# Ranks in the delta stage, fetches at the ends of the down projection's chains, and work moved to GpSimd and ScalarE in a hybrid decoder layer

## The chip, the cores and the metric

The kernel runs on 1 core of one Trainium2 chip. The metric is the device time of one execution, in microseconds (us). Engines are named as in the profile: PE is TensorE's matmul side and PEld its weight loads, DVE is VectorE, ACT ScalarE, POOL GpSimd, SP the engine that issues most DMAs. Each engine works through its instructions in one fixed order; an instruction whose operands aren't ready holds up what is behind it on its engine.

## The reference

One layer of a hybrid decoder over 1024 prompt rows and 8 sample rows, D_MODEL 1024, D_FF 2816, all in f32:

```python
h = _rmsnorm(x, norm1_w) * (1 + sc1) + sh1
qkv, gdn_gate, beta_raw, a_raw, sq, sk, sv, ga, gb = _split_in(h @ w_in)
# delta rule, 8 heads of 128, chunks of 64: t_inv = inverse of (I + M) per chunk,
# then a scan over chunks with the state S:
v_new = u_n - w_n @ S
o = qd_n @ S + a_n @ v_new
S = S * last_n + kd_n.T @ v_new
y_a = _gdn_out(o_a, gdn_gate, gdn_onorm_w) @ w_gdn_out
y_b = o_b @ w_swa_out                      # o_b: sliding-window attention
x = x + gt1 * ((sigmoid(ga) * y_a + sigmoid(gb) * y_b) @ w_o)
h2 = _rmsnorm(x, norm2_w) * (1 + sc2) + sh2
gc = _causal_dwconv(h2 @ w_ffn_gate, ffn_conv_w) + ffn_conv_b
x = x + gt2 * ((silu(gc) * (h2 @ w_ffn_up)) @ w_ffn_down)
```

A final RMSNorm follows, and the new states are outputs too.

## The kernel before

Every f32 matmul is made of three: each operand is split into a high part (a rounded copy, made on ACT, L127) and a low part (the rest, made on DVE, L128), and `mm3` issues high by high, low by high and high by low (L178, L179, L180). So each weight that is fetched passes ACT and DVE before PE can use it. Rows stand in three parts of 384, 384 and 264 (`PARTS`) or in quarters of 256 and 260, features in the 128 partitions.

The stages follow one another: modulation and first norm to about 45 us; attention to 430; the delta stage to 1150; the branches (the products with w_swa_out and w_gdn_out, and the sample rows' delta step) to 1330; the output pass (w_o), woven with the second norm and the FFN's operands, to 1445; gate and up to about 1885; down to 2090; the tail with the final norm.

**Order.** The program is written as generators, and `weave` (L1248) gives each one a start and a step: before each piece is written out the priority is set to the stream's start, plus its step for every piece so far. A scheduler then fixes the order on each engine: of what it takes to be ready, the instruction of the lowest priority number goes first. `weave` also says where the next weave begins (`end`).

**Delta stage.** For each head h, `run` (L1924) weaves the inverse (`unit_inverse`, L980), the scan over the chunks (`delta_scan`, L916), the preparation of the next head, and work that only fills: `head_projections` (L797) makes the gate of head h (three tiles) and q, k, v of head h+2 (nine tiles) in two PSUM banks, and `pieces` (L805) draws from one generator that makes first the branch gates (`gates`, L1271; tiles of 24 matmuls in one PSUM bank, taken out on ACT at L1284, written to the DRAM buffers sgb and sga) and then the part of w_swa_out's product that is ready early (`early_out`, L1294). The inverse of a head ends in a chain: L1046 on PE, copies L1048 on ACT, L1051 on PE, L1053 and L1055 on ACT, L1057 on DVE, L1060 on PE, L1061 on ACT, L1064 on PE, L1065 on ACT. A step of the scan is L937 (PE), L938 (DVE), L940 (PE), L942 (ACT), L944 (PE), L953 (DVE), with the outputs at L947 and L948. `early_out` fetches the attention's output (ob) part 2 for itself, and part 0 (`obX`) for the branches; both fetches are split piece by piece on ACT (b1h) and on DVE.

**Branches** (`branches`, L1318). Tiles rotate through five PSUM banks by `next_mm` (`self.turn`). A tile of w_gdn_out's product is multiplied by its gate rows (L1331) and added (L1332); the gate rows are fetched by `gate_part` (L1374) from sga, for the last products into two buffers `sgx`. DVE also makes the sample rows' state updates there (L1207, eight in a row).

**Output pass and second norm.** The loads of w_o (L1431) stand on SP behind those of `gate_part`. `second_norm` (L1462) takes a root on POOL (L123), makes a diagonal on DVE (L1488) and spreads it with PE (L1489). `ffn_states` (L1538) transposes the stored FFN rows (L188). `pair_weights` (L1560) fetches 2 x 2 blocks of an FFN weight and forms the seven operands of Strassen's scheme; its sums (L1572) run on POOL, except for the first blocks of gate and up, on DVE.

**Gate and up** (`ffn_gate_up`, L1636). `conv` (L1657) makes the causal convolution of a gate tile: one multiply with a bias (L1662), then DVE steps (L1664) and the activation.

**Down** (`ffn_down`, L1709). Seven Strassen products of eleven steps each are run in the chains (5, 3), (4, 7), (1), (2) and (6). Within a chain the products go on in the same eight PSUM banks, and `take` (L1763) copies the sums out after each product (L1766, on ACT). `fetch` brings a step's operands 13 steps ahead: DMAs, for most products a sum on POOL (L1737), then the split on ACT and DVE.

## Time and profile before

| | |
|---|---|
| time, median of 3 runs | 2136.81 us (2132.54 to 2142.25) |
| the profiled execution's own time | 2136.28 us |
| its span | 2134.5 us |
| mean granted PE clock | 0.979 |
| PE, DVE, ACT, POOL busy | 96%, 65%, 40%, 25% of the span |
| DMA | 274.95 MB, mean 129 GB/s |

A row of the timeline has the start (us), the duration (us), the engine and line, operation, output and inputs, shape and count; behind it in brackets stand the engine's idle time before that row and what released it. A row of the waits has the total us, the number of times and the longest. Busy time of PE includes the time in which pipelined matmuls overlap, so it says where PE stood still, not how well it was used.

### The profile page before, as it was taken

To read this page: it belongs to the slowest core of one execution; us is meant where nothing else is said; L and a number is where in the kernel's file an instruction comes from. 1 tells how busy PE (TensorE), PEld (TensorE's weight loads), DVE (VectorE), ACT (ScalarE), POOL (GpSimd) and SP (SyncE) were. 2 spreads that over 40 slices of the span, in tenths; PEclk is the share of its full clock that TensorE was granted. 3 is DMA by queue.
4 is the path that set the end of the run, shared out by engine and by line. 5 is a ranking of instruction groups with operands and counts; after the bars stand their busy time and mean duration, and the time that the engine had idled before them with its cause. 6 is when DMAs were issued, how large, how long until landed. Compare 5 with 4: busy or idle time off the path is not lost. (4 is left out here: it accounts for less than half of the span.)

```text
span 2134.5 us, 41210 instructions
## 1 busy us (share of the span) xinstructions
PE 2046.5 (96%) x16245; PEld 1935.3 (91%) x16245; DVE 1393.5 (65%) x2781; ACT 854.7 (40%) x2125; POOL 534.6 (25%) x592
## 2 busy tenths in 40 slices
PE   7999999999899999999989989998999999999898
PEld 4985888899899999999879989898999999999898
DVE  4756667465655736557445575479888788678866
ACT  3655445434244233443343222344343343343443
POOL 1000000020221211212110220003546546545531
PEclk8999999999999999999989999999999999999999
DMA  7256442141332322313166663622333333388972
GB/s 272 86 133 204 141 161 90 49 135 48 76 85 58 83 58 54 89 52 76 48 183 211 213 224 100 182 61 71 109 95 95 110 95 95 120 285 276 317 228 85
DMA packets 301821, 274.95 MB, mean 129 GB/s; under 512 B 59666, under 2 KB 248303, under 8 KB 301612
## 3 DMA queue, kind: packets, MB, share of 16 engines
q1 hardware_dynamic: 296140, 252.49, 38.6%
q0 software_dynamic: 5200, 19.32, 2.6%
q8 instruction: 127, 2.08, 0.4%
q14 instruction: 66, 0.54, 0.1%
q10 hardware_dynamic: 288, 0.52, 0.1%
HBM read 212.54 MB, written 62.12 MB: 129 GB/s over the span
## 5 line engine op out<-in xcount | busy, mean ns | idle before, releaser
L178 PE MATMUL mm<-b1h,wh 128*128 128x384 f32 (+1 forms) x1520 | 499.0, 329 | 5.9 <-ACT gt L1284 4.1
L180 PE MATMUL mm<-b1h,wl 128*128 128x384 f32 (+1 forms) x1520 | 491.4, 325 | 2.1 <-DVE wl L128 2.1
L179 PE MATMUL mm<-b1l,wh 128*128 128x384 f32 (+1 forms) x1520 | 490.8, 323 | 0.0
L178 PEld LDWEIGHTS mm<-b1h,wh 128*128 128x128 f32 x1520 | 287.8, 190 | 15.7 <-ACT gt L1284 6.2
L180 PEld LDWEIGHTS mm<-b1h,wl 128*128 128x128 f32 x1520 | 287.3, 189 | 7.9 <-issue 4.3
L179 PEld LDWEIGHTS mm<-b1l,wh 128*128 128x128 f32 x1520 | 288.0, 189 | 3.8 <-issue 3.5
L127 ACT ACTIVATE wh<-raw 128x1024 fp32r<-128x1024 f32 x83 | 87.0, 1048 | 135.7 <-PE mm L179 75.9
L128 DVE TENSOR_TENSOR wl<-raw,wh 128x1024 fp32r<-128x1024 f32 x82 | 100.8, 1229 | 48.8 <-ACT wh L127 47.9
L179 PE MATMUL mm<-pk,w 128*128 128x260 f32 (+1 forms) x440 | 124.3, 283 | 1.1 <-DVE pk L128 1.1
L178 PE MATMUL mm<-pk,w 128*128 128x260 f32 (+1 forms) x440 | 124.3, 283 | 0.0
L180 PE MATMUL mm<-pk,w 128*128 128x260 f32 (+1 forms) x440 | 124.2, 282 | 0.0
L128 DVE TENSOR_TENSOR w<-ws,w 128x512 fp32r<-128x512 f32 x88 | 74.1, 843 | 37.4 <-ACT w L127 37.4
L1609 ACT COPY bml<-mm 128x256 f32<-128x256 f32 (+1 forms) x132 | 49.2, 374 | 108.5 <-PE mm L180 101.8
L178 PE MATMUL mm<-bmh,w 128*128 128x260 f32 (+1 forms) x320 | 90.4, 283 | 0.9 <-DVE fa L1686 0.9
L180 PE MATMUL mm<-bmh,w 128*128 128x260 f32 (+1 forms) x320 | 90.3, 282 | 0.0
L180 PE MATMUL mm<-b2h,wl 128*128 128x384 f32 (+1 forms) x256 | 83.4, 329 | 4.5 <-DVE wl L128 4.5
L178 PE MATMUL mm<-b2h,wh 128*128 128x384 f32 (+1 forms) x256 | 83.8, 329 | 2.4 <-DVE t L1327 2.4
L179 PE MATMUL mm<-b2l,wh 128*128 128x384 f32 (+1 forms) x256 | 83.9, 328 | 0.4 <-DVE b2l L128 0.4
L179 PEld LDWEIGHTS mm<-pk,w 128*128 128x128 f32 x440 | 82.8, 188 | 1.3 <-DVE pk L128 1.3
L178 PEld LDWEIGHTS mm<-pk,w 128*128 128x128 f32 x440 | 82.8, 188 | 0.3 <-ACT bml L1609 0.2
L180 PEld LDWEIGHTS mm<-pk,w 128*128 128x128 f32 x440 | 83.0, 189 | 0.0
L127 ACT ACTIVATE w<-ws 128x512 fp32r<-128x512 f32 x88 | 55.4, 632 | 49.9 <-PE wv L180 45.0
(648 smaller groups left out, 5984.1 us busy)
## 6 DMA issues: line engine op xcount, KB each, us to landing
raw<-in_w_in_dram SPq DMA_DIRECT2D x60, 512.0 KB
ws<-in_w_ffn_down_dram SPq DMA_DIRECT2D x55, 256.0 KB
raw<-xd SPq DMA_DIRECT2D x47, 258.0 KB
raw<-in_w_ffn_down_dram SPq DMA_DIRECT2D x47, 256.0 KB
raw<-in_w_ffn_gate_dram SPq DMA_DIRECT2D x22, 512.0 KB
raw<-in_w_ffn_up_dram SPq DMA_DIRECT2D x22, 512.0 KB
qst<-in_w_mod_dram SPq DMA_DIRECT2D x16, 512.0 KB
raw<-in_w_mod_dram SPq DMA_DIRECT2D x16, 512.0 KB
```

What stands on the lines that cost most here:

```text
L127: self.nc.scalar.activation(hi, x, AF.Copy)
L128: (eng or self.nc.vector).tensor_tensor(lo, x, hi.bitcast(F32), op=ALU.subtract)
L178: mm(ps, whi, xhi, start=first, stop=False, **kw)
L179: mm(ps, whi, xlo, start=False, stop=False, **kw)
L180: self.last_mm = mm(ps, wlo, xhi, start=False, stop=last, **kw).ins
L1609: self.last_copy = nc.scalar.copy(r[p, i], x[p])
```

## The change

It has nine edits. (1) `weave` counts only streams of step 1 for `end`. (2) In the delta stage the streams of `head_projections`, and for head 6 that of the last gates, start at 100000 instead of 500 or 600, behind the 10000 of the pieces. (3) `early_out` loads ob part 0 at its fourth round instead of ahead of the first. (4) `gate_part` issues the `sgx` loads from POOL's queue. (5) The convolution's first step is an ACT activation. (6) In `ffn_down` fetches don't run in the last two steps of a chain's last product, and the splits of fetches from the 13th on are ordered behind the last copy. (7) `ffn_states` starts at 460 instead of 300. (8) The sums of the first gate block run on POOL. (9) `branches` begins with the first bank of the rotation. Line numbers after the change are one higher from L1303 on, and two or more from L1738 on.

```diff
         for gen, start, step in streams:
             at = tc.cur_priority = p + start
             for _ in gen:
-                if start < 10000:
+                if step == 1:
                     end = max(end, tc.cur_priority)
                 at += step
                 tc.cur_priority = max(at, tc.cur_priority) if step == 1 else at
-            if start < 10000:
+            if step == 1:
                 end = max(end, tc.cur_priority)
         tc.cur_priority = end
 
...
         self.S0, states = [], [self.flat_room(self.b1, "b1", x, 1) for x in "hl"]
         X = {2: self.load_part(self.b1, self.ob, 2, "b1")}
         w = load(0)
-        self.obX = {0: self.load_part(self.b1, self.ob, 0, "b1")}
         for j in range(8):
             s = self.t(self.gt[0], [P, 384], self.gt[1])[:, :n]
             nc.sync.dma_start(s, self.sgb[j][:, lo:lo + n])
...
                 nc.vector.tensor_tensor(s, ps, s, op=ALU.mult)
                 nc.sync.dma_start(self.ubd[j], s)
 
+            if j == 3:
+                self.obX = {0: self.load_part(self.b1, self.ob, 0, "b1")}
             now, w = w, load(j + 1) if j < 7 else None
             if j < 6:
                 self.load_state(j, states[j // 3])
...
 
     def gate_part(self, pool, src, t):
         s = (self.t(pool, [P, 384], "gt") if pool is self.gt[0] else self.t(pool, [P, 384], "sgx", bufs=2))[:, :PARTS[t][1]]
-        self.nc.sync.dma_start(s, src)
+        (self.nc.sync if pool is self.gt[0] else self.nc.gpsimd).dma_start(s, src)
         return s
 
 
...
             e = min(c + n, NP)
             zi, ai = z[i], a[i]
             col = lambda j: fcw[:, j, f + i:f + i + 1]
-            nc.vector.tensor_scalar(ai[:, c:e], zi[:, 2 + c:2 + e], col(2), col(3), op0=ALU.mult, op1=ALU.add)
+            nc.scalar.activation(ai[:, c:e], zi[:, 2 + c:2 + e], AF.Identity, scale=col(2), bias=col(3))
             for j in (0, 1):
                 nc.vector.scalar_tensor_tensor(ai[:, c:e], zi[:, j + c:j + e], col(j), ai[:, c:e],
                                                op0=ALU.mult, op1=ALU.add)
...
                 1: ((0, 0, 1), (1, 1, 1)), 2: ((0, 1, 1), (1, 1, -1)), 6: ((1, 1, 1),)}
         steps = [(i, g) for c in chains for i in c for g in range(G)]
         ready, waiting = {}, ([], [])
+        self.took = None
         less = []
 
         def fetch(s):
...
             room = self.room(tags[s % len(tags)], [P, KC * QW])
             hi, lo = room[:, :n + 512], room[:, n + 512:2 * (n + 512)]
             with ExitStack() as after:
-                if 5 <= s < len(tags):
-                    for ins in (self.last_up, self.last_copy):
-                        after.enter_context(self.tc.issue_after(ins.ins))
+                for ins in (self.last_up, self.last_copy) if 5 <= s < len(tags) else (self.took,) if s >= len(tags) and self.took else ():
+                    after.enter_context(self.tc.issue_after(ins.ins))
                 self.split(hi, lo, raw)
             ready[s] = hi, lo
             if s == 5:
...
         def take(ps, i, p, j):
             self.turn = (self.turn + 1) % KC
             r = self.copies[:, self.turn, :256 + 4 * p]
-            nc.scalar.copy(r, ps)
+            self.took = nc.scalar.copy(r, ps)
             for k, h in enumerate(home[i]):
                 waiting[k].append((r, p, j, *h))
 
         banks = [(self.pmm, "mm", 2), (psum, "wv", 2), (psum, "wy", 2)] * 2 + [(self.pmf, "mm", 1), (psum, "nr", 1)]
         order = [(p, j) for j in range(4) for p in range(2)]
         s = done = 0
+
+        def fetch_to(n):
+            nonlocal done
+            while done < min(n, len(steps)):
+                fetch(done)
+                done += 1
+
         for c in chains[:-1]:
             ps = {(p, j): self.t(pl, [P, 512], tag, bufs=k)[:, :256 + 4 * p] for (p, j), (pl, tag, k) in zip(order, banks)}
             for i in c:
                 for g in range(G):
-                    while done < min(s + len(tags), len(steps)):
-                        fetch(done)
-                        done += 1
+                    if i != c[-1] or g < G - 2:
+                        fetch_to(s + len(tags))
                     for p, j in order:
                         step(s, ps[p, j], p, j, g == 0 and i == c[0], g == G - 1, {"skip_group_check": True} if i != c[0] else {})
                         if g == G - 1:
...
                     s += 1
         for x in waiting[0] + waiting[1]:
             add(*x)
-        while done < len(steps):
-            fetch(done)
-            done += 1
+        fetch_to(len(steps))
         self.ffn_rows(pool, psum)
         tail = self.norm_rows(pool, psum, [2 * P, 3 * P])
         chunks = [[0], [P], [], [], [4 * P, 5 * P], [6 * P, 7 * P, NP], [], []]
...
                     self.squares, self.X, self.wo = {}, {}, []
                     norm = lambda q: self.second_norm(xr, psum, q)
                     self.weave((chain(*(self.output_pass(xr, q) for q in range(4))), 0, 1),
-                               (self.ffn_states(xr, psum), 300, 30),
+                               (self.ffn_states(xr, psum), 460, 30),
                                (chain(norm(0), self.operands(xr, 0, 0)), 250, 10),
                                (chain(norm(1), self.operands(xr, 0, 1)), 490, 20),
                                (chain(norm(2), self.operands(xr, 1, 0)), 730, 120))
                 with S() as left:
                     pool = self.pool("pf", 1, ctx=left)
-                    w = self.pair_weights(pool, self.I["w_ffn_gate"][0], 0, nc.vector)
+                    w = self.pair_weights(pool, self.I["w_ffn_gate"][0], 0)
                     last, ops = norm(3), self.operands(xr, 1, 1)
                     self.weave((chain(islice(last, 3), islice(ops, 1), last, ops), -100, 1))
                     right.close()
...
                     streams = [(self.unit_inverse(pool, psum, h, prep[0]), 0, 1),
                                (self.delta_scan(pool, psum, h, prep), 100, 1)]
                     if h + 2 < H:
-                        streams[1:1] = [(chain(self.pieces(2), self.head_projections(pa, pool, h)), 500, 100)]
+                        streams[1:1] = [(chain(self.pieces(2), self.head_projections(pa, pool, h)), 100000, 100)]
                         streams.append((self.pieces(3), 10000, 100))
                     else:
                         if h + 2 == H:
-                            streams[1:1] = [(chain(self.pieces(3), *(self.delta_gate(pa, pool, i) for i in (h, h + 1))), 500, 1)]
-                        streams.append((self.head_projections(pa, pool, h), 600, 100))
+                            streams[1:1] = [(chain(self.pieces(3), *(self.delta_gate(pa, pool, i) for i in (h, h + 1))), 100000, 100)]
+                        streams.append((self.head_projections(pa, pool, h), 100000, 100))
                     if h + 1 < H:
                         streams.append((self.delta_prepare(pool, psum, h + 1), 250, 1))
                     self.weave(*streams)
...
             pool2, pool = self.pool("p6b", 1, ctx=c), self.pool("p6", 1, ctx=c)
 
             self.psm, more = self.pool("qs", 2, PSUM, ctx=c), self.pool("qb", 2, PSUM, ctx=c)
-            mm, self.mm = self.mm, [self.pmm, self.pmm, self.pmf, more, more]
+            mm, self.mm, self.turn = self.mm, [self.pmm, self.pmm, self.pmf, more, more], -1
             self.branches(pool, pool2)
             self.mm = mm
         cg.close()
```

The change moves instructions on every engine. Three places show how. Each piece is unbroken; the numbers in the names only tell tiles apart.

**PE, the last head's inverse.** tp, T, MR, UZ and W are the inverse's tiles (names 12xxx, L1046 to L1064), rc and vn the scan's, mm_12339 a tile of `early_out`. Before:

```order
L1046 MATMUL tp_12088<-MR_12010,U_1902_11947 32x32 x16
L178 MATMUL mm_12339<-b1h_1987_12296,wh_12312 128x264
L179 MATMUL mm_12339<-b1l_1988_12297,wh_12312 128x264
L180 MATMUL mm_12339<-b1h_1987_12296,wl_12313 128x264
L1051 MATMUL tp_12090<-T_12005,tmp_12089 32x32 x16
L1060 MATMUL tp_12130<-MR_12010,UZ_11948 64x64 x8
L1064 MATMUL tp_12140<-W_4463,UZ_11948 64x64 x8
L940 MATMUL rc_12153<-vn_11914,W_4463 128x128
L178 MATMUL mm_12339<-b1h_1987_12296,wh_12312 128x264
```

After, from the same L1046 on (mm_11700 and mm_11735 are gate tiles, rc_11516 to o_11463 belong to the scan of head 6):

```order
L1046 MATMUL tp_12088<-MR_12010,U_1902_11947 32x32 x16
L940 MATMUL rc_11516<-y_11512,W_4463 128x128
L178 MATMUL mm_11700<-b1h_14_152,wh_11638 128x264
L179 MATMUL mm_11700<-b1l_15_153,wh_11638 128x264
L180 MATMUL mm_11700<-b1h_14_152,wl_11639 128x264
L178 MATMUL mm_11700<-b1h_14_152,wh_11638 128x264
L179 MATMUL mm_11700<-b1l_15_153,wh_11638 128x264
L180 MATMUL mm_11700<-b1h_14_152,wl_11639 128x264
L1051 MATMUL tp_12090<-T_12005,tmp_12089 32x32 x15
L944 MATMUL rc_11520<-s_11518,kd_10802 128x128
L948 MATMUL o_11463<-s_11518,A_10854 128x128
L1051 MATMUL tp_12090<-T_12005,tmp_12089 32x32
```

and at L1060:

```order
L179 MATMUL mm_11735<-b1l_15_153,wh_11731 128x264
L180 MATMUL mm_11735<-b1h_14_152,wl_11732 128x264
L178 MATMUL mm_11735<-b1h_14_152,wh_11731 128x264
L179 MATMUL mm_11735<-b1l_15_153,wh_11731 128x264
L1060 MATMUL tp_12130<-MR_12010,UZ_11948 64x64 x8
L180 MATMUL mm_11735<-b1h_14_152,wl_11732 128x264
L178 MATMUL mm_11735<-b1h_14_152,wh_11731 128x264
L179 MATMUL mm_11735<-b1l_15_153,wh_11731 128x264
```

Before, three matmuls of another stream stand between L1046 and L940; now gate tiles and the last step of head 6's scan stand between its steps.

**ACT, the same place.** b1h are the splits of ob (b1h_1987 part 2, b1h_1992 part 0 before, b1h_2008 part 0 after), gt the gate tiles' way out. Before:

```order
L127 ACTIVATE b1h_1987_12296<-b1l_1988_12297 128x528 x2
L127 ACTIVATE b1h_1992_12316<-b1l_1993_12317 128x768
L127 ACTIVATE wh_12406<-raw_12404 128x1024
L1284 ACTIVATE gt_11818<-mm_11793 128x384
L127 ACTIVATE b1h_1992_12316<-b1l_1993_12317 128x768
L1048 COPY tmp_12089<-tp_12088 32x256 x2
L127 ACTIVATE b1h_1992_12316<-b1l_1993_12317 128x768 x2
L1053 COPY w_1927_12125<-tp_12090 32x256
L1055 COPY W_4463<-tp_12090 32x8x32 x2
L1061 COPY UZ_11948<-tp_12130 64x512
L1065 COPY W_4463<-tp_12140 64x8x64
L942 ACTIVATE s_12155<-rc_12153,c_1887_11877 128x128
```

After:

```order
L1061 COPY UZ_11948<-tp_12130 64x512
L1284 ACTIVATE gt_11760<-mm_11735 128x264
L127 ACTIVATE b1h_1987_12296<-b1l_1988_12297 128x528 x3
L1065 COPY W_4463<-tp_12140 64x8x64
L127 ACTIVATE b1h_1987_12296<-b1l_1988_12297 128x528
L1284 ACTIVATE gt_11789<-mm_11764 128x384
L127 ACTIVATE b1h_2008_12426<-b1l_2009_12427 128x768 x2
L942 ACTIVATE s_12155<-rc_12153,c_1887_11877 128x128
L127 ACTIVATE wh_12392<-raw_12390 128x1024
L1284 ACTIVATE gt_11818<-mm_11793 128x384
L127 ACTIVATE b1h_2008_12426<-b1l_2009_12427 128x768 x2
L942 ACTIVATE s_12168<-rc_12166,c_1887_11877 128x128
```

The copies of the inverse (L1048 stands 10 rows above this piece) are now ahead of the splits of part 0, and these stand ahead of the first two L942 of the last scan.

**SP and POOL, the end of the branches.** On SP before:

```order
L1543 DMA out_dram<-in_state_ffn_conv_dram 8x2816
L1376 DMA sgx_14157<-sga_3915 128x384
L1376 DMA sgx_14190<-sga_3915 128x384
L1376 DMA sgx_14223<-sga_3915 128x264
L1376 DMA sgx_14256<-sga_3915 128x264
L1431 DMA raw_14296<-in_w_o_dram 128x8x128
L1431 DMA raw_14334<-in_w_o_dram 128x8x128
L1431 DMA raw_14370<-in_w_o_dram 128x8x128
```

On SP after:

```order
L1544 DMA out_dram<-in_state_ffn_conv_dram 8x2816
L1432 DMA raw_14296<-in_w_o_dram 128x8x128
L1432 DMA raw_14334<-in_w_o_dram 128x8x128
L1432 DMA raw_14370<-in_w_o_dram 128x8x128
L1415 DMA x_2197_14293<-xT_949 128x256 x6
```

and on POOL after, with the first sums of the FFN's gate weight and the second norm's root (rs):

```order
L1377 DMA sgx_14157<-sga_3915 128x384
L1377 DMA sgx_14190<-sga_3915 128x384
L1377 DMA sgx_14223<-sga_3915 128x264
L1377 DMA sgx_14256<-sga_3915 128x264
L1573 TENSOR_TENSOR ws_15483<-raw_15473,raw_15475 128x512
L1573 TENSOR_TENSOR ws_15485<-ws_15483,raw_15473 128x512
L1573 TENSOR_TENSOR ws_15493<-raw_15473 128x512
L123 TENSOR_TENSOR rs_15356<-rs_15356,mhalf 128x2
```

The loads of w_o no longer have the four gate loads ahead of them, and three weight sums stand ahead of the root on POOL, where before only the root stood.

## The prediction

> **What bounds the kernel now.** I read the page's busy lines first, then busy time in stretches of 50 us, then PE's waits, then the timeline around each place where PE stands idle.
>
> ```profile
> span 2134.5 us, 41210 instructions
> PE 2046.5 (96%) x16245; PEld 1935.3 (91%) x16245; DVE 1393.5 (65%) x2781; ACT 854.7 (40%) x2125; POOL 534.6 (25%) x592
> PE   7999999999899999999989989998999999999898
> ```
>
> PE is busy 96% of the span, so no other engine's total matters. The change removes no matmul and adds none, so all it can win or lose lies in the 2134.5 - 2046.5 = 88 us in which PE is idle, and in slow matmuls behind idle time. About 15 of the 88 us stand in the first slice, ahead of everything that is edited. The rest is spread over places of 0.4 to 5 us. The question of each edit is therefore which of those places it closes, and which it opens.
>
> In the next view a row is a stretch: its length, busy us (instructions) of PE, PEld, DVE, ACT, POOL, then the granted PE clock, the DMA share and GB/s.
>
> ```profile
> 550.00:600.00 50.00, 45.97 (x482) 42.82 (x481) 22.80 (x60) 18.38 (x54) 10.07 (x15) 1.00 0.27 78
> 1100.00:1150.00 50.00, 41.01 (x364) 39.19 (x363) 24.57 (x43) 20.33 (x45) 3.84 (x5) 0.86 0.74 217
> 1450.00:1500.00 50.00, 43.86 (x352) 42.36 (x352) 47.57 (x67) 22.62 (x44) 24.88 (x23) 1.00 0.25 78
> 1700.00:1750.00 50.00, 50.00 (x422) 50.00 (x421) 38.09 (x67) 19.69 (x40) 28.27 (x28) 1.00 0.35 109
> ```
>
> Head 0 of the delta stage loses 4.0 us in its 50, the end of the delta stage 9.0, the start of the FFN 6.1 with DVE at 47.57 of 50. In the middle of the FFN PE never stops.
>
> **The delta stage: the ranks (A and B).** The longest idle time there stands in the last head's inverse, a chain PE, ACT, PE, DVE, PE, ACT, PE, ACT, PE:
>
> ```profile
> 1108.00 1.45 PE L1051 MATMUL tp<-T,tmp 32*32 32x32 f32 x32 [4.15 <-ACT tmp L1048]
> 1112.19 1.94 PE L1060 MATMUL tp<-MR,UZ 64*64 64x64 f32 x16 [2.75 <-DVE MR L1057]
> 1114.80 1.96 PE L1064 MATMUL tp<-W,UZ 64*64 64x64 f32 x16 [0.67 <-ACT UZ L1061]
> 1117.43 0.80 PE L940 MATMUL rc<-vn,W 128*128 128x128 f32 x2 [0.67 <-ACT W L1065]
> ```
>
> That is 4.15 + 2.75 + 0.67 + 0.67 = 8.2 us. By the order of the instructions nothing but three matmuls stands between these steps before, because the last gate tiles were all used up ahead of them; after, dozens of gate matmuls stand between L1046 and L1064. ACT explains the 4.15:
>
> ```profile
> 1104.66 0.84 ACT L127 ACTIVATE b1h<-b1l 128x768 fp32r<-128x768 f32 x1 [2.70 <-DMA b1l<-ob]
> 1107.58 0.75 ACT L1048 COPY tmp<-tp 32x256 f32<-32x256 f32 x2
> 1109.75 0.84 ACT L127 ACTIVATE b1h<-b1l 128x768 fp32r<-128x768 f32 x1 [0.47 <-DMA b1l<-ob]
> ```
>
> The copies of L1048 stood behind splits of the attention's output that waited for their DMA. After the change these splits (the later load of ob part 0) stand behind L1065, but ahead of the first two L942 of the last scan. So the 8.2 us go, and the 2.70 + 0.47 = 3.2 us of waiting for the DMA turn up in the scan, at most. I charge them in full; if the load lands later still, I allow 7.
>
> The idle time has a tail. The same 264-wide matmul takes 0.42 us right behind it and 0.28 us three us later, and the granted clock of this stretch is 0.86, against 1.00 in its neighbours:
>
> ```profile
> 1118.24 0.42 PE L179 MATMUL mm<-b1l,wh 128*128 128x264 f32 x1
> 1120.68 0.28 PE L178 MATMUL mm<-b1h,wh 128*128 128x264 f32 x1
> ```
>
> If the slow clock is half the full one, 0.86 means (1 - 0.86) x 50 / 0.5 = 14 us of it. Of these, 8.2 us were idle; PE lost half of the other 5.8, that is 2.9 us. The Trainium skill ("TensorE: Matmul & The Clock Gate", Part 1) says that the array falls to half its clock after an idle window of about 3.4 us and needs about as long a busy one to come back. This trace agrees in kind behind 4.15 us, though a shorter gap (2.75 us at 1230.23, below) is also followed by a matmul of 0.69 us, where the same shape takes 0.41 and 0.44 in the two rows under it. By the page's figures one slow window of 3.4 us would cost 1.7 us and the sum would be 1.2 us smaller; I keep the 2.9 of the row.
>
> **B: -8.2 - 2.9 + 3.2 = -7.9 us** (from -11.1 to -4).
>
> **A** is heads 0 to 6. Here PE waits mostly for a gate tile's way out of the one PSUM bank that the fillers share:
>
> ```profile
> PE mm L178 <- ACT gt L1284: 4.1, 7, 1.3
> ```
>
> Seven waits, 4.1 us in total, the longest 1.3. They arise where one gate tile follows another with little between. Counted in the order of the instructions, 16 of 39 tiles stand so before and 9 after, because at head 0 projections now alternate with gate tiles. With one wait for a weight's low half,
>
> ```profile
> 546.58 0.45 PE L180 MATMUL mm<-b1h,wl 128*128 128x384 f32 x1 [1.40 <-DVE wl L128]
> ```
>
> 5.5 us are to be had; by the count, 7/16 of them go. **A: -2 us** (from -5 to +6, if the bunched projections wait in their two banks instead).
>
> **Branches (C).** A reset rotation of the five banks and the moved operands:
>
> ```profile
> 1230.23 0.69 PE L180 MATMUL mm<-b2h,wl 128*128 128x384 f32 x1 [2.75 <-DVE wl L128]
> 1237.97 0.41 PE L178 MATMUL mm<-b2h,wh 128*128 128x384 f32 x1 [2.35 <-DVE t L1327]
> 1261.40 0.44 PE L180 MATMUL mm<-b2h,wl 128*128 128x384 f32 x1 [1.74 <-DVE wl L128]
> ```
>
> The first is the same in both orders: the weight's low half stands behind eight state updates on DVE. At the second a tile of 24 matmuls of another part now stands ahead of the one that waits for its bank, so the 2.35 goes. At the third the low half moved ahead on DVE, but other updates still precede it, so I take half. **C: -2.35 - 0.9 = -3.2 us** (from -6 to +2).
>
> **Gate rows through GpSimd, FFN states later (D).**
>
> ```profile
> 1311.00 12.80 SPq L1376 DMA_DIRECT2D sgx<-sga  x4
> 1323.85 2.08 SPq L1431 DMA_DIRECT2D raw<-in_w_o_dram  x3
> 1330.12 0.39 PE L1422 MATMUL mm<-bmh,w 128*128 128x256 f32 x1 [2.06 <-ACT w L127]
> 1342.80 0.39 PE L180 MATMUL mm<-bmh,pk 128*128 128x256 f32 x1 [0.75 <-DVE pk L128]
> 1349.38 0.39 PE L180 MATMUL mm<-bmh,pk 128*128 128x256 f32 x1 [0.64 <-DVE pk L128]
> 1353.58 0.52 PE L188 MATMUL wv<-ident,raw 88*128 88x88 f32 x4 [0.78 <-DMA raw<-in_state_ffn_conv_dram]
> ```
>
> SP sits 12.80 us in four gate loads whose two buffers come free tile by tile, and the first three loads of w_o are queued behind. On POOL the same loads block nothing, since it does nothing at all in this stretch:
>
> ```profile
> 1300.00:1350.00 50.00, 46.55 (x335) 45.92 (x334) 26.79 (x53) 14.99 (x32) 0.00 (x0) 1.00 0.56 158
> ```
>
>  The w_o loads then wait only for their own buffers, some 13 us earlier, and the next ones find the DMA rings emptier. The state's transposes are ranked later, behind more of the output pass. **D: -2.06 - 0.75 - 0.64 - 0.78 = -4.2 us** (from -5 to 0: if POOL brings a gate row late, the tile's bank stays taken, at most the 2.35 us of the bank that DVE kept at 1237.97, and the state's 0.78 stays).
>
> **Weight sums on GpSimd (E).**
>
> ```profile
> 1364.26 0.69 DVE L1572 TENSOR_TENSOR ws<-raw,raw 128x512 f32<-128x512 f32 x1 [6.80 <-DMA raw<-in_w_ffn_gate_dram]
> 1366.89 0.72 POOL L123 TENSOR_TENSOR rs<-rs,mhalf 128x2 f32<-128x2 f32 x1 [105.45 <-issue]
> 1368.12 0.70 PE L1489 MATMUL nr<-dg,ones 128*128 128x256 f32 x2 [2.77 <-DVE dg L1488]
> L1572 POOL TENSOR_TENSOR ws<-raw,raw x20: 1280/1346/1713, 1465.6 to 1843.0; 128x512 f32<-128x512 f32 x20
> ```
>
> DVE stood 6.80 us in front of a sum whose weight was on its way, and the second norm behind it. Now POOL stands there, three sums ahead of the root L123 that the norm needs. The load is queued on SP behind the same stores, which follow PE, so it lands at the same place in the program: the root comes 3 x 1.35 = 4.0 us after the landing, against 1366.89 - 1364.26 = 2.6 us before. PE has 14 more matmuls ahead of L1489 in the new order, 14 x 0.12 = 1.7 us at the 50 us per 422 matmuls of the row 1700. The stall stays at about 2.5 us. **E: 0** (from -2.8 to +3).
>
> **FFN gate and up (F).** The first step of the convolution goes from DVE to ACT.
>
> ```profile
> 1484.67 0.38 PE L178 MATMUL wv<-bml,w 128*128 128x256 f32 x1 [1.60 <-DVE bml L1684]
> 1491.61 0.39 PE L178 MATMUL mm<-bmh,w 128*128 128x260 f32 x1 [0.72 <-DVE fa L1686]
> 1494.93 0.39 PE L178 MATMUL wv<-pk,w 128*128 128x260 f32 x1 [1.38 <-DVE bml L1684]
> L1662 DVE TENSOR_SCALAR fa<-fz,fcw 128x512 f32<-128x512 f32 x4 | 2.1, 537 | 0.0
> L127 ACT ACTIVATE w<-ws 128x512 fp32r<-128x512 f32 x88 | 55.4, 632 | 49.9 <-PE wv L180 45.0
> ```
>
> In the first stretch DVE is nearly full and 1.60 + 0.72 + 1.38 = 3.7 us of PE's idle time end with it. Four steps of 0.54 us leave DVE there, 2.1 us, so I let 2.0 of the 3.7 go. Over the stage 44 x 0.54 = 24 us leave DVE and, at the 632 ns of an activation of this size, 28 us come to ACT. PE covers both: from 1500 on it is full while ACT has 30 us free in 50 (the row 1700). Were that cover gone, a step of 0.63 against 0.54 would lengthen each of 44 chains by 0.1 us, 4 us. **F: -2.0 us** (from -3.7 to +4).
>
> **The down projection (G).**
>
> ```profile
> 1985.46 1.06 ACT L127 ACTIVATE bmh<-bmh 128x1028 fp32r<-128x1028 f32 x1 [2.42 <-POOL bmh L1737]
> 1986.84 0.58 PE L178 MATMUL mm<-pk 128*128 128x256 f32 x1 [4.98 <-ACT bml L1766]
> 2021.60 0.39 PE L178 MATMUL mm<-bml 128*128 128x256 f32 x1 [1.28 <-ACT bml L1766]
> ```
>
> The copies out of PSUM stand behind splits that wait for their fetch. But the 4.98 us fall at the end of product 4, the first of the chain (4, 7), and the edit holds fetches back only in the last product of a chain; before the copies of product 4 the same two splits stand in both orders. At the end of product 7 one split still stands among the copies, now one copy earlier. The names say that the stall at a chain's end goes; the order says that it doesn't. **G: 0** (from -9, the 6.3 shown and a slow tail like B's 2.9, to +5, one more such stall).
>
> **The sum.** -2 - 7.9 - 3.2 - 4.2 + 0 - 2.0 + 0 = -19.3 us. The profiled execution took 2136.28 us (1.8 of it outside the span), 0.5 below the median of 2136.81, so I forecast **2117 us**.
>
> **The rivals.**
>
> - *The down stalls go as well* (chance 0.10). For it: the splits wait for POOL, so a fetch that comes 2.42 us earlier frees the copies. Against it: the order above. 2117 - 9 = 2108.
> - *The stalls move on* (0.18). Engines work in order; what is no longer late lets the next thing be late. The last scan waits 7 us for ob part 0 (B: -4.1), A and C give 0, E costs 3, F gives 0, D half of its 4.2. That is -3.2: 2133. For it: the splits that set L1048 free now stand ahead of L942 on the same ACT; against it: PE has filler in the new order at each place.
> - *Slower: projections ranked last* (0.07). A head makes three gate and nine projection tiles, so 72 over six heads. If they bunch at a head's end behind all other work, each turn waits for a bank as gate tiles do now, 4.1/7 = 0.59 us: 72 x 0.59 = 42, less the 17.3 of the other terms: 2161. From 0.24 us a turn the gain is gone, from 0.39 it is slower by over 0.5%. For it: the rank stands behind even the fillers; against it: two banks instead of one, and orders that hardly differ from head 1 to 5.
> - *The change doesn't do what it says* is counted in G, at nothing.
>
> **How the numbers follow.** The forecast has 0.65, with a range of its own from 2105 to 2130. About 0.5% (10.7 us) is what a measurement of this kernel can tell from no change: faster is below 2126, slower above 2147. Of the 0.65 I put 0.57 below 2126, with the 0.10 of the down stalls and 0.03 of the stalls that move on: 0.70. Slower is 0.07, the rest, 0.23, is the same. For 8 in 10 I leave out the slower rival and the ends of the others: 2103 to 2137.
>
> **What the profile after would show.** B right: no gap over 1 us at L1051 and L1060 of the last head and a granted clock near 1.00 there; wrong: a gap at L940 or L944 ended by ACT s L942. A: the waits for gt fall from seven to about four; wrong: waits of projections for z or th. C: no 2.35 in front of a part's first matmul. D: the w_o loads on SP stand some 13 us ahead of their first use, no gap at L1423. E: the gap of 2 to 3 us at the second norm stays, now ended by POOL. F: DVE under 47 of 50 between 1450 and 1500 in the program's place. G: one stall of about 5 us still in front of product 7. What would make all of it wrong: PE idle above 88 us in total.

## The result and the profile after

The changed kernel takes 2119.37 us (median of 6 runs, 2113.12 to 2124.07) against 2134.27 us of the kernel before beside it (6 runs): a ratio of 0.9922, 95% interval 0.9898 to 0.9946. A second comparison on another chip gave 2118.41 against 2137.03 us, a ratio of 0.9909 (0.9893 to 0.9925). The forecast was 2117 us, or 0.991. The medians differ by 14.9 and by 18.6 us; the two profiled executions, of which all that follows is read, by 2134.5 - 2115.2 = 19.3 us of span. So the size of the gain is known to some 4 us.

The page of the changed kernel:

```profile
span 2115.2 us, 41270 instructions
PE 2041.3 (97%) x16245; PEld 1929.9 (91%) x16245; DVE 1358.7 (64%) x2733; ACT 883.5 (42%) x2169; POOL 535.6 (25%) x602
```

PE's idle time falls from 88.0 to 2115.2 - 2041.3 = 73.9 us, 14.1 less. Its busy time falls by 5.2 us although the matmuls are the same; I take this for time at the slow clock, as the mean granted clock rose from 0.979 to 0.984. Together they make the 19.3 us of the span.

Three of the stretches that the prediction shows, and one in the down projection (us, then busy us of PE, PEld, DVE, ACT, POOL, granted clock, DMA share, GB/s):

```profile
550.00:600.00 50.00, 48.14 (x490) 46.12 (x489) 29.98 (x66) 17.07 (x41) 11.30 (x16) 1.00 0.31 81
1100.00:1150.00 50.00, 45.51 (x343) 43.41 (x340) 27.23 (x49) 19.72 (x42) 7.45 (x10) 1.00 0.90 259
1450.00:1500.00 50.00, 49.27 (x412) 49.06 (x411) 44.87 (x66) 23.90 (x49) 31.27 (x29) 1.00 0.31 93
1950.00:2000.00 50.00, 45.73 (x361) 45.52 (x361) 35.73 (x36) 21.76 (x27) 32.48 (x20) 0.93 0.91 313
```

Head 0 has 2.2 us more of PE in its 50, the end of the delta stage 4.5 and the full clock, the start of the FFN 5.4. The down projection still stops, and its granted clock of 0.93 is that of before.

A stretch holds other work in the two kernels, so I cut both at the same matmuls instead: the delta stage from the first L1028 to the last L944, the branches to the first matmul of w_o, the output pass to the last spreading of the norm (L1489 before, L1490 after), gate and up to the first matmul of the down projection, and down to the end of the span. All are start times in PE's timeline.

| stage (us) | before | after | difference | of it PE idle | forecast |
|---|---|---|---|---|---|
| ahead of the delta stage | 494.0 | 496.3 | +2.3 | +0.7 | 0 |
| delta stage | 651.2 | 641.7 | -9.5 | -7.3 | A and B: -9.9 |
| branches | 184.9 | 181.4 | -3.4 | -0.8 | C, and D's 2.06: -5.3 |
| output pass | 115.4 | 112.3 | -3.1 | -1.5 | the rest of D, and E: -2.1 |
| gate and up | 453.1 | 448.9 | -4.2 | -3.1 | F: -2.0 |
| down and tail | 235.8 | 234.5 | -1.3 | -2.1 | G: 0 |

PE's idle time in a stage is the stage's length less PE's busy time in it; the remainder of each difference is matmuls that ran faster or slower. D's 2.06 us stand in front of the first matmul of w_o, so by this cut they count with the branches.

The sum of -19.3 us is the forecast's own. That it fits so well is chance, as the rows and the experiments show: terms missed in opposite directions, and the first line, which the change doesn't touch, moved too.

PE's rows at the last inverse, in order of the program:

```profile
1087.32 0.69 PE L1046 MATMUL tp<-MR,U 32*32 32x32 f32 x32
1094.24 1.14 PE L1060 MATMUL tp<-MR,UZ 64*64 64x64 f32 x16
1105.39 0.38 PE L940 MATMUL rc<-vn,W 128*128 128x128 f32 x2
```

No bracket stands behind them: PE had filler work up to each. L1060 takes 1.14 us, where it took 1.94 before at the slow clock.

### The profile page after: what moved, and what is told of

It reads as the page before. It is cut to its first block, busy times and chain, and to the rows that moved or that the text cites. A ratio compares the mean times of both kernels' runs of the same rounds, so it can differ in the third digit from the quotient of the medians.

```text
span 2115.2 us, 41270 instructions
## 1 busy us (share of the span) xinstructions
PE 2041.3 (97%) x16245; PEld 1929.9 (91%) x16245; DVE 1358.7 (64%) x2733; ACT 883.5 (42%) x2169; POOL 535.6 (25%) x602
## 4 chain that ended last, share of the span: by engine, by line
PE 76%; DMA 8%; DVE 7%; ACT 2%; issue 2%; POOL 2%; SPq 1%; DVEq 0%; POOLq 0%; ACTq 0%
PE mm L178 17%; PE mm L180 17%; PE mm L179 17%; PE wv L178 2%; PE wv L180 2%; PE wv L179 2%; DMA ws<-in_w_ffn_down_dram 1%; PE wy L178 1%; PE wy L180 1%; PE wy L179 1%; PE pv L645 1%; DMA raw<-in_w_ffn_down_dram 1%; PE tp L188 1%; PE mm L262 1%; PE pv L643 1%
## 5 line engine op out<-in xcount | busy, mean ns | idle before, releaser
L1665 DVE SCALAR_TENSOR_TENSOR fa<-fz,fcw,fa 128x512 f32<-128x512 f32 x88 | 73.5, 854 | 18.4 <-ACT fa L1663 18.1
```

The lines of the kernel that those rows point to most:

```text
L1665: nc.vector.scalar_tensor_tensor(ai[:, c:e], zi[:, j + c:j + e], col(j), ai[:, c:e], op0=ALU.mult, op1=ALU.add)
```

## The experiments

In each kernel the stages are cut as above, from one profile each. Where kernels have the same code in a stage, its length still differs: the branches of the changed kernel, of its repetition and of five variants that leave them alone run from 181.4 to 184.6 us, with PE busy from 172.9 to 175.9. So a difference under 3 us in the branches, seen once, shows nothing. Gate and up are steadier, 448.9 us in six kernels that leave them alone. `obx_back`, `turn_back`, `sgx_sp`, `sums_dve`, `conv_dve` and `down_back` were run once each, and their times, 2114.48 to 2122.88 us, lie within the changed kernel's own spread: they are read by stages alone.

### The ranks or the later load

`ranks_back` is the changed kernel with edits 1 and 2 undone:

```diff
-                        streams[1:1] = [(chain(self.pieces(2), self.head_projections(pa, pool, h)), 100000, 100)]
+                        streams[1:1] = [(chain(self.pieces(2), self.head_projections(pa, pool, h)), 500, 100)]
...
-                        streams.append((self.head_projections(pa, pool, h), 100000, 100))
+                        streams.append((self.head_projections(pa, pool, h), 600, 100))
```

> The changed kernel with the ranks of the delta stage (edits 1 and 2) as before; ob part 0 is still loaded at the fourth round. The delta stage, from the first L1028 to the last L944 on PE, took 651.2 us before and 641.7 after. Theory A (the ranks close the gaps, because gate tiles are left over for the last inverse): the stage is back at 647 to 651 us, with 4 us or more of gaps between the last L1046 and L940, and the whole 6 to 9 us slower than the changed kernel. Rival B (the later load of ob part 0 does it, because the copies L1048 no longer stand behind its splits): the stage stays at 641 to 644 us and the last inverse has under 2 us of gaps.

2131.45 us against 2138.93 of before, 0.9973 (0.9958 to 0.9988). The delta stage takes 653.6 us, longer than either expectation, and PE's timeline has the old stalls again:

```profile
1110.32 1.45 PE L1051 MATMUL tp<-T,tmp 32*32 32x32 f32 x32 [4.35 <-ACT tmp L1048]
1114.00 1.94 PE L1060 MATMUL tp<-MR,UZ 64*64 64x64 f32 x16 [2.23 <-DVE MR L1057]
1116.61 1.96 PE L1064 MATMUL tp<-W,UZ 64*64 64x64 f32 x16 [0.67 <-ACT UZ L1061]
```

The later load doesn't free the copies by itself. On ACT the splits of part 0 (128x768) still stand ahead of L1048, one of them waiting for its DMA:

```profile
1106.99 0.84 ACT L127 ACTIVATE b1h<-b1l 128x768 fp32r<-128x768 f32 x1 [1.90 <-DMA b1l<-ob]
1109.91 0.75 ACT L1048 COPY tmp<-tp 32x256 f32<-32x256 f32 x2
```

`ranks_only` is the other side, the kernel before with edits 1 and 2 alone.

> The kernel before with only the ranks of the delta stage changed (edits 1 and 2). Theory A (the ranks do it): the delta stage takes 641 to 645 us against 651.2 before, all other stages are as before, and the whole is 7 to 10 us faster than before. Rival B (the later load of ob part 0 is needed): 647 us or more and a whole within 4 us of before.

2125.65 us, 0.9941 (0.9924 to 0.9958): 12.6 us, more than expected. The delta stage takes 642.5 us. Other stages moved too, where the edit isn't: in its profile the output pass takes 110.8 us, 4.6 less than before, and the part ahead of the delta stage 498.8, 4.8 more.

`obx_back` takes back edit 3 alone.

```diff
+        self.obX = {0: self.load_part(self.b1, self.ob, 0, "b1")}
         for j in range(8):
...
-            if j == 3:
-                self.obX = {0: self.load_part(self.b1, self.ob, 0, "b1")}
```

> The changed kernel with ob part 0 loaded ahead of the loop of early_out, as before; the new ranks stay. Theory A (the ranks do it): the delta stage stays at 641 to 644 us (641.7 after). Rival B (the later load does it): 646 us or more, with a gap of 2.7 us or more in front of the last L1051.

The delta stage stays at 641.3 us, the last inverse has no gap. The three kernels agree: the ranks make the gain of the delta stage and the later load none of it. They do it in two ways. PE has other work during the chain, and the copies L1048 no longer stand behind splits. They wait for PE alone, in `obx_back` as in `ranks_only` and the changed kernel, here `obx_back`:

```profile
1084.79 0.76 ACT L1048 COPY tmp<-tp 32x256 f32<-32x256 f32 x2 [1.68 <-PE tp L1046]
```

The 4.15 us in front of L1051 and the 2.75 in front of L1060, ahead of which two splits stood as well, could have gone by either way, and no run separates them. The two gaps of 0.67 us have no split ahead of them, so there it is the work beside the chain.

### The rotation of the banks

```diff
-            mm, self.mm, self.turn = self.mm, [self.pmm, self.pmm, self.pmf, more, more], -1
+            mm, self.mm = self.mm, [self.pmm, self.pmm, self.pmf, more, more]
```

> The changed kernel without the reset of the bank rotation in the branches (edit 9). From the last L944 to the first matmul of the output pass 184.9 us before, 181.4 after. Theory (the reset sets the order in which tiles take banks, and so closes the 2.35 and 1.74 us): 183.5 us or more, the gap of 2.35 in front of L178 is back. Rival (the order there follows from the ranks and the load that moved, the reset does nothing): 180.5 to 182.5 us.

The branches take 188.8 us, outside the spread of the others, and the waits at the three places of the prediction are back on PE:

```profile
1226.17 0.44 PE L180 MATMUL mm<-b2h,wl 128*128 128x384 f32 x1 [2.46 <-DVE wl L128]
1233.96 0.66 PE L178 MATMUL mm<-b2h,wh 128*128 128x384 f32 x1 [2.15 <-DVE t L1328]
1256.71 0.44 PE L180 MATMUL mm<-b2h,wl 128*128 128x384 f32 x1 [1.08 <-DVE wl L128]
```

In the changed kernel the same three places read:

```profile
1224.26 0.44 PE L180 MATMUL mm<-b2h,wl 128*128 128x384 f32 x1 [2.56 <-DVE wl L128]
1232.00 0.41 PE L178 MATMUL mm<-b2h,wh 128*128 128x384 f32 x1 [0.76 <-DVE t L1328]
1237.65 0.44 PE L178 MATMUL mm<-b2h,wh 128*128 128x384 f32 x1 [1.36 <-ACT wh L127]
```

The first stays, as forecast. The 2.35 shrinks to 0.76 and the 1.74 is gone, but a wait of 1.36 for a weight's high half is new, and one of 1.03 at 1151.23. The reset does close the wait for the bank (L1328, L1327 before): without it 2.35 us before, 3.78 in `ranks_only` and 2.15 here; in the eleven kernels with it 0.76 once and otherwise nothing. It isn't shown to be worth the 7.3 us by which this stage is longer here. Only 2.3 of them are idle time (10.8 against 8.5 us); the others are slower matmuls (granted clock 0.97 against 1.00), and the output pass gives 2.2 back (110.1 against 112.3).

### Gate rows and sums through GpSimd

```diff
-        (self.nc.sync if pool is self.gt[0] else self.nc.gpsimd).dma_start(s, src)
+        self.nc.sync.dma_start(s, src)
```

> The changed kernel with the late gate rows issued from SP again (edit 4 back). The output pass, from the first L1423 to the last L1490, took 115.4 us before and 112.3 after; the gap in front of the first L1423 was 2.06 in both. Prediction's step D (the queue on SP makes the first weights of w_o late): the pass is 1.4 us or more longer than after. Theory now (the first gap is the path of the last tile through DVE and ACT, and the weights were there in time): the gap is 2.06 again, the pass within 1.0 us of 112.3 and the stage before it within 0.5 us.

The gap is 2.06 us a third time, so the queue on SP never made it. The pass takes 114.0 us and the branches 183.6, 1.7 and 2.1 more than in the changed kernel and more than I expected. But `obx_back`, which has edit 4, takes 113.9 us in its pass, and branches with edit 4 take up to 184.6 us. Nor is PE idle for longer: 2.9 us in the pass and 8.8 in the branches, against 3.5 and 8.5 in the changed kernel. What is longer is matmuls at a slower clock. So no run shows a gap that edit 4 closes, and its reason is refuted.

```diff
-                    w = self.pair_weights(pool, self.I["w_ffn_gate"][0], 0)
+                    w = self.pair_weights(pool, self.I["w_ffn_gate"][0], 0, nc.vector)
```

> The changed kernel with the first gate block's weight sums on DVE again (edit 8 back). Prediction's step E (POOL's three sums are as long as the wait that DVE had): the output pass within 0.7 us of 112.3. Theory now (the sums on DVE held up the second norm and the clock fell behind the gap of 2.77): 113.5 to 115 us, a gap of 2.4 to 3 in front of L1490 or the granted clock under 1.00 between 1350 and 1400.

113.2 us, between the two expectations, a gap of 1.95 us in front of L1490 (1.70 with the sums on POOL). The edit can't be seen: the same gap is 1.14 us in `ranks_only`, with the sums on DVE, and 2.43 in `obx_back`, with the sums on POOL. In the changed kernel POOL reads as E had it, here with the spreading that waits for it:

```profile
1352.41 1.29 POOL L1573 TENSOR_TENSOR ws<-raw,raw 128x512 f32<-128x512 f32 x1 [38.62 <-DMA raw<-in_w_ffn_gate_dram]
1353.77 1.29 POOL L1573 TENSOR_TENSOR ws<-ws,raw 128x512 f32<-128x512 f32 x1
1355.02 1.28 POOL L1573 TENSOR_TENSOR ws<-raw 128x512 f32<-128x512 f32 x1
1356.26 0.72 POOL L123 TENSOR_TENSOR rs<-rs,mhalf 128x2 f32<-128x2 f32 x1
```

```profile
1357.49 0.70 PE L1490 MATMUL nr<-dg,ones 128*128 128x256 f32 x2 [1.70 <-DVE dg L1489]
```

The root starts 1356.26 - 1352.41 = 3.85 us after the weight has landed (forecast 4.0), queued behind three sums that it doesn't need.

### The convolution on ACT

```diff
-            nc.scalar.activation(ai[:, c:e], zi[:, 2 + c:2 + e], AF.Identity, scale=col(2), bias=col(3))
+            nc.vector.tensor_scalar(ai[:, c:e], zi[:, 2 + c:2 + e], col(2), col(3), op0=ALU.mult, op1=ALU.add)
```

> The changed kernel with the convolution's first step on DVE again (edit 5 back). From the last L1490 to the first matmul of the down projection 453.1 us before, 448.9 after. Theory (DVE was the bound of the first 40 us of gate and up, and 2.1 us of its work leave): 451 to 453 us, gaps in front of L178 ended by DVE L1685 or L1687 of 2 us or more together. Rival (the sums that left DVE, edit 8, made the room): under 450 us.

Gate and up take 453.1 us again, as before to a hundredth, the sums on POOL notwithstanding. PE's waits are back at the three places, the last two at their old length and the first at 0.35 instead of 1.60 us:

```profile
1469.86 0.39 PE L178 MATMUL wv<-bml,w 128*128 128x256 f32 x1 [0.35 <-DVE bml L1685]
1476.81 0.39 PE L178 MATMUL mm<-bmh,w 128*128 128x260 f32 x1 [0.74 <-DVE fa L1687]
1480.13 0.39 PE L178 MATMUL wv<-pk,w 128*128 128x260 f32 x1 [1.38 <-DVE bml L1685]
```

With the step on ACT one of them is left, 0.73 us:

```profile
1470.00 0.38 PE L178 MATMUL wv<-bml,w 128*128 128x256 f32 x1 [0.73 <-DVE bml L1685]
```

So edit 5 is worth 4.2 us, and edit 8 none of it: in `sums_dve`, without edit 8, the stage takes 449.2 us.

### The down projection

`down_back` has the fetches as before.

```diff
-                    if i != c[-1] or g < G - 2:
-                        fetch_to(s + len(tags))
+                    fetch_to(s + len(tags))
...
-                for ins in (self.last_up, self.last_copy) if 5 <= s < len(tags) else (self.took,) if s >= len(tags) and self.took else ():
+                for ins in (self.last_up, self.last_copy) if 5 <= s < len(tags) else ():
```

> The changed kernel with the fetches of the down projection as before (edit 6 back). From the first matmul of the down projection to the end of the span 235.8 us before, 234.5 after, the stall at product 4's end 4.98 and 4.27. Prediction's step G (the edit does nothing there): 234 to 236 us, the stall between 4 and 5.5. Rival (the edit holds the splits back from the copies at product 7's end): 235.5 us or more, with gaps of 1.28 and 0.58 again at product 7's end.

234.7 us against 234.5, and the stalls read 4.47 and 0.48 where the changed kernel has

```profile
1968.12 0.58 PE L178 MATMUL mm<-pk 128*128 128x256 f32 x1 [4.27 <-ACT bml L1767]
2003.00 0.39 PE L178 MATMUL mm<-bml 128*128 128x256 f32 x1 [0.45 <-ACT bml L1767]
```

Edit 6 does nothing that shows, as G said.

`hold_first` carries the edit to where the stall is: fetches stop after the fourth step of a chain's first product.

```diff
-                    if i != c[-1] or g < G - 2:
+                    if g < (G - 2 if i == c[-1] else 4):
```

> The changed kernel with one condition of the down projection widened: in a chain's first product fetches stop after the fourth step and go on in the next product, so that on ACT no lagging split stands ahead of the copies L1767 of products 5 and 4. Theory (those splits alone make the stall of 4.3 to 5.3 us in front of product 7): the stall falls under 1 us, the down stage from 234.5 to about 229 to 231 us, the clock stays at 1.00 behind it. Rival (the operands of product 7 are late as well, the stall only moves into product 7 or to its end): the stage stays at 233.5 us or more, with a new wait of PE for a split of bmh, pk or bml.

Half of each. The copies of product 4 stand free and PE has no gap in front of product 7, but at the end of product 7 PE's timeline has

```profile
2003.67 0.58 PE L178 MATMUL mm<-bml 128*128 128x256 f32 x1 [8.18 <-ACT bml L1767]
```

and the stage takes 236.7 us, the whole 2118.74 us, 0.9914 (0.9896 to 0.9932) against 0.9909 of the changed kernel beside it (`after_again`). The stall isn't made by the order of splits and copies alone. The fetches run behind: the DMA engines are 0.92 busy from 1950 to 2000 here, and the splits are held up by POOL's sums, which wait for the fetches (4.47 us in front of the sum at 1979.05). Here the next in line behind a late split pays.

> The changed kernel as it is, for a comparison on the same chip as the next three. 0.990 to 0.995 of the kernel before.

It came out at 0.9909.

### The last scan

In the last head's scan after the change PE waits where it didn't before. The waits of PE from 1100 to 1140 (total us, times, longest):

```profile
PE rc L940 <- DVE y L938: 3.9, 4, 1.6
PE rc L944 <- ACT s L942: 0.5, 1, 0.5
```

DVE's rows show what is ahead of L938:

```profile
1119.46 0.43 DVE L1308 TENSOR_TENSOR gt<-mm,gt 128x264 f32<-128x264 f32 x1 [2.07 <-DMA gt<-sgb]
1119.81 0.34 DVE L938 SCALAR_TENSOR_TENSOR y<-rc,d,vn 128x128 f32<-128x128 f32 x1
```

A product of `early_out` waits there for its gate rows, and the DMA engines are 0.90 busy from 1100 to 1150 (0.74 before): it seems that the same loads now fall into less time. `states_later` moves six loads of 512 KB, the sample rows' states, from `early_out` into the branches.

```diff
-            if j < 6:
-                self.load_state(j, states[j // 3])
...
+        for j in range(6):
+            load(j, self.states[j // 3])
         load(6, c)
         load(7, c)
```

> The changed kernel with the loads of the sample rows' six states (512 KB each) moved from early_out to the sample step in the branches. In the last head's scan PE waited 4.5 us for DVE y L938, which stood behind L1308 and its gate rows while the DMA engines were full. Theory (the loads crowd the scan): the gaps in front of L940 in the last scan fall under 2 us together and the delta stage from 641.7 to 639 us or less; the branches may pay up to 4 us. Rival (the scan without its last filler is simply a chain of waits): the same 4 to 4.5 us of gaps.

The theory holds for the waits of the scan: those for L938 are gone, 1.3 us for L942 and 0.4 for L966 are left. The delta stage takes 640.3 us, where I expected 639 or less. And the branches take 193.0 us, 11 more, with a new wait behind the loads,

```profile
1157.64 1.01 PE L178 MATMUL mm<-b2h,wh 128*128 128x384 f32 x2 [6.45 <-ACT b2h L127]
```

and the whole is 2124.55 us, 0.9942 (0.9925 to 0.9959), slower than the changed kernel: 2122.74 to 2127.51 us in four runs against 2115.01 to 2120.53 in five of the changed kernel beside it.

> hold_first and states_later in one. If both theories hold: 5 to 8 us faster than the changed kernel; if the branches pay for the states: as hold_first.

2126.31 us, 0.9948 (0.9934 to 0.9962), 7.9 us slower than the changed kernel beside it: the two moved stalls add up. No version here is shown to beat the changed kernel.

## Why the prediction was right, and where it wasn't

**Delta stage (A and B): right, with one part of its working wrong.** -9.5 us against -9.9, shown by three kernels to be the ranks. The waits for gate tiles fell as A had it:

```profile
PE mm L178 <- ACT gt L1284: 2.0, 5, 0.6
```

from 4.1 to 2.0 us. In B the 8.2 us of gaps went. The slow clock behind them went too: 24.9 - 17.6 = 7.3 us of the stage's gain are idle time, so 2.2 of the 9.5 are faster matmuls, where B had 2.9. Slow spells in other heads came and went as well, so this is no proof of the step. The 3.2 us that I charged to the scan came, 4.4 in PE's waits, but not as I said: but for 0.5 us it is not ACT's L942 behind splits of ob, but DVE's L938 behind gate rows that the crowded DMA engines brought late. I had looked for what the moved load would hold up, and not for what the emptied gaps would do to the DMA engines.

**Branches (C): the wait right, the number in part luck.** The reset closes the wait for the bank. But PE's idle time in the stage fell by 0.8 us only, because new waits stand in place of old ones, and by C and D together it should have fallen by 5.3. The other 2.6 of the 3.4 us are faster matmuls, before and then after:

```profile
1145.24:1330.12 184.88, 175.59 (x1172) 172.13 (x1170) 110.47 (x247) 46.42 (x98) 28.59 (x23) 0.98 0.59 187
1137.97:1319.41 181.44, 172.94 (x1171) 169.47 (x1169) 109.44 (x247) 46.12 (x98) 32.19 (x29) 1.00 0.62 192
```

PE's busy time in this stage differs by as much between kernels with the same code.

**Output pass (D): the step failed.** I put the 2.06 us in front of w_o's first matmul down to the queue on SP. It is there in each of the 14 kernels, to the hundredth, although SP now takes up the loads of w_o early:

```profile
1293.21 12.30 SPq L1432 DMA_DIRECT2D raw<-in_w_o_dram  x3
```

ACT's rows of the changed kernel:

```profile
1318.32 0.52 ACT L127 ACTIVATE bmh<-t 128x4 fp32r<-128x4 f32 x2 [2.38 <-DVE t L1333]
1318.74 1.13 ACT L127 ACTIVATE w<-raw 128x512 fp32r<-128x512 f32 x2
```

and of the kernel before, which the prediction doesn't show:

```profile
1329.03 0.52 ACT L127 ACTIVATE bmh<-t 128x4 fp32r<-128x4 f32 x2 [2.38 <-DVE t L1332]
1329.45 1.14 ACT L127 ACTIVATE w<-raw 128x512 fp32r<-128x512 f32 x2
```

In both the weight's split follows the last tile's split with no idle time between: it waits for its place on ACT, not for its DMA. Ahead of it runs the path of the last tile, PE to DVE to ACT, which no queue shortens. The next two weights' splits did wait for their DMA before, 0.27 and 0.79 us, but in `sgx_sp`, with the old queue, they don't. The other 0.75 and 0.64 us came back as 0.58, 0.76 and 0.34. Only the state's 0.78 went, and even that returns in kernels with the same edit (0.81 in `hold_first`); no run takes back edit 7 alone. And `ranks_only`, which has none of edits 4, 7 and 8, has an output pass of 110.8 us. So the 3.1 us that the stage gained aren't shown to be D's. The kernel before was long there for a reason that its own rows show in part, the 2.77 of the norm and a slow spell behind it (granted clock 0.76 from 1368 to 1375), and that these edits didn't have to remove. Why `ranks_only` lost it stays open.

**Weight sums (E): right about POOL** (3.85 us from landing to root, 4.0 forecast). The stall shrank from 2.77 to 1.70 us, where I had 2.5; the 1.95 of `sums_dve` and the 1.14 of `ranks_only`, both with the sums on DVE, show that it shrinks without the edit.

**Gate and up (F): the mechanism right, its size forecast at half.** I took the DVE work that leaves the stretch, 2.1 us, as the bound of the gain. 3.0 of the 3.7 us of gaps closed, and the stage is 4.2 us shorter, beyond F's own lower end of -3.7: 3.1 are idle time, the rest faster matmuls. `conv_dve` takes the 453.11 us of before although PE's gaps add up to 2.5 us in it, not 3.7, which fits that DVE sets the length. That a step of DVE stands ahead of others several times over, so that taking it out is worth more than its own time, is my reading and not tested. The full gaps were the better bound.

**Down (G): right.** The edit's words promise a chain's end; the order showed that the stall stands in the middle of one and that the same splits precede the copies. `hold_first` shows that this reordering wouldn't have helped: the fetches are late.

**The sum** is right by luck in its parts. What fell short (0.4 us in the delta stage, 1.9 in the branches, where D's 2.06 stayed, and 2.3 lost ahead of the delta stage) is nearly what came beyond the forecast (1.0 in the output pass, 2.2 in gate and up, 1.3 in the down projection). The loss ahead of the delta stage isn't the change's: the matmuls of the attention come in the same order in both kernels and ran with less clock, and over the 14 profiles the part ahead of the delta stage takes from 492.1 to 498.8 us. Granted clock from 350 to 430, before and then after:

```profile
350.00:430.00 80.00, 75.72 (x456) 64.35 (x454) 39.08 (x129) 37.18 (x131) 3.25 (x5) 0.89 0.14 46
```

```profile
350.00:430.00 80.00, 75.73 (x435) 64.16 (x435) 39.10 (x129) 36.18 (x129) 3.23 (x5) 0.85 0.14 46
```

PE is as busy in both, and gets 21 matmuls less done.

## What to carry to other kernels

A wait's releaser is only the last link: before a gap is put down to a queue, look at the releasing engine's own row, and if no idle time stands in front of it, the queue isn't late. Filler work is worth most where a chain has nothing beside it, so rank it to be left over there; but look at the loads that come with it, for here the next wait was theirs. Where a stream of fetches runs behind, an order that spares one victim can pick another, as here. And before a stage's gain is credited to an edit, split it into idle time and faster matmuls, and look at a stage that the edits don't touch.

## What the runs showed of the hardware that was not expected

Slow spells of PE's clock differ from run to run of the same instructions: with 0.89 against 0.85 granted in 80 us of attention, its last product of values (L645) starts at 425.99 instead of 423.24 us, 2.75 later, more than most of the edits above are worth. The same gap can be followed by a slow spell or not. Behind 2.06 us of idle time in front of w_o's first matmul the granted clock from 1321 to 1326 was 0.72 in `sgx_sp` and 1.00 in the changed kernel, and the same matmuls took 0.41 and 0.28 us. Behind a stall of 4.27 us a matmul of 256 columns took 0.58 us at first, as behind 4.98 and 8.18; the size of the stall doesn't show in it.
